# Expert weights of a pair side by side: 2 MB transfers, nine ring buffers, two one-time buffers

## The chip, the cores and the metric

The kernel runs on one core of a Trainium2 chip. The metric is device time in microseconds (us) of one execution. Seven units matter: TensorE (PE; PEld is its weight load), VectorE (DVE), ScalarE (ACT), GpSimd (POOL), SyncE (SP, which here only issues DMAs), and 16 DMA engines that all queues share.

## The reference, cut to what matters

One decoder layer over 576 tokens (512 prompt, 64 sample): a mixer, cross-attention, and a hierarchical mixture of experts, which is the part that is changed. All of it is float32.

```python
def hier_moe(x, w_gr, b_gr, w_er, b_er, w_e1, w_e3, w_e2):
    g_idx = argmax(x @ w_gr + b_gr)                  # one of 4 groups per token
    top_l, top_i = top_k(logits of the group's 8 experts, 2)
    gate = p_g * softmax(top_l)
    ...
    # per expert: (silu(xb @ w_e1[e]) * (xb @ w_e3[e])) @ w_e2[e]
    # rows are weighted by gate and added to their tokens
...
y = rmsnorm(h + hier_moe(rmsnorm(h, g3)), g_final)
```

There are 32 experts; w_e1 and w_e3 are 1024x512, w_e2 is 512x1024, so an expert has 6 MB of weights and all of them 192 MB (201 million bytes). With 576 tokens nearly every expert is used, and all are read.

## The kernel before, in words

Up to about 580 us the kernel computes mixer and cross-attention; the last projection (`w_co`, its weights in the tiles `wst`) runs from 518 to 578 us. Then it routes: logits, ranks, places (lines 1082 to 1274). The tile `more`, which says whether any expert overflows its 64 slots, is written at the end of that. Tokens are written to a DRAM table `rows_d`, and fetched back sorted by group with indirect DMAs (`fetch_rows`, line 1061) into `acc`, two tiles of 128 rows for each group; `acc` has room for two groups.

The experts run in 16 pairs of two (loop at line 1564), four pairs to a group. Of a pair p:

- `gather` (line 1493) makes X, the pair's tokens by features, with one-hot matmuls from `pthi`, `ptlo`, which `split_group` (line 1477) makes of the fetched rows: a rounded part on ACT and the rest on DVE, in four blocks of columns.
- First products, line 1575: 32 matmuls of X with w_e1 and w_e3 into two banks H. Each expert takes 64 of the 128 output rows, so the two experts' matmuls alternate. A matmul is two records in the profile.
- The gate, lines 1597 to 1600: Silu on ACT, a multiplication on DVE, into `sg`. TensorE turns `sg` (line 1603), ACT copies it (line 1607).
- Second products, line 1616: 16 matmuls with w_e2 into Y, which is split into `yhi`, `ylo`; `combine` (line 1528) adds them to `acc` through one-hot matmuls, one pair later.

Every four pairs a group is finished: final norm, and an indirect store to `y`. At pair 9 (`GENERAL`) stands a branch on `more` over code for overflowing experts, which the given inputs do not take.

Weights come through SP's queue in the order of use: 12 transfers of 1 MB for a pair (`load_one`, line 1308). Transfers 0 to 7 are the quarters of w_e1|w_e3, of one expert and then of the other; 8 to 11 the halves of w_e2. Each of the 128 partitions receives a row of 8 KB. They go into a ring of 18 buffers, 13 in the pool `wpa`, which is free from 518 us, and 5 in `wpb`, which is free when the last projection ends. The last three of the first 18 also wait for the first fetched rows (`i_first`). From then on a transfer waits until the products have read the buffer that it reuses. The last pair's w_e2 is loaded as four column blocks, each by two transfers of 512 KB in rows of 256 numbers (line 1328); the last pair is also worked off in these blocks, with the last norm between them (`last_norm`, line 1543).

A scheduler orders the instructions of each engine by their place in the program and by their dependences; `tc.issue_after(i)` keeps an instruction behind i on the engine's queue. An engine works its queue off in order. SP also reads `more` into a register (a TENSOR_LOAD, line 1448), at the place in its queue where the scheduler puts it.

In this text a **unit** is 2 MB of weights: the two experts' transfers of the same quarter or half. A pair has six units, the kernel 96, numbered 0 to 95. Before the change a unit is two transfers; the ring holds nine units.

Of the kernel before, what the change touches and what calls it, by code (L numbers as in the profile page):

```python
# [21 lines left out]
T = 576  # L22
# [5 lines left out]
CHUNK_A, CHUNK_B = 13, 5  # L28
PAY = 24
GENERAL = 9  # L30
CUT = 128
# [67 lines left out]
def _lay_out(inputs):  # L99
# [49 lines left out]
    w13 = np.concatenate([f["w_e1"][0], f["w_e3"][0]], 2).reshape(32, 4, 2, 128, 1024)  # L149
    a["w13"] = ca(w13.transpose(0, 1, 3, 2, 4)).reshape(32, 4, 128, 2048)  # L150
    w2 = f["w_e2"][0].reshape(32, 4, 128, 2, 512)
    a["w2"] = ca(w2.transpose(0, 3, 2, 1, 4)).reshape(32, 2, 128, 2048)
# [23 lines left out]
def body(ctx: ExitStack, tc: tile.TileContext, I, O, dbg=None):  # L176
# [847 lines left out]
    acc = keep.tile([128, 4, D], F32, name="acc")  # L1024
# [57 lines left out]
    with ExitStack() as st:  # L1082
        rp = pool(st, "route")
        space = acc.rearrange("p a c -> p (a c)")
        acc3, last = space[:, 0:T], space[:, T:2 * T]
        gp.memset(space[:, 2 * T:2048], 0.0)
        gp.memset(space[64:128, 3584:4096], 0.0)
        stage = [space[:, 2048 + i * 512:2560 + i * 512].rearrange("p (i c) -> p i c", c=128) for i in range(3)]
        stage4 = space[0:64, 3584:4096]
        hots = [space[:, a:a + 320].bitcast(BF16).rearrange("p (i c) -> p i c", c=128) for a in (2048, 3072)]  # L1090
# [115 lines left out]
        i_first = [fetch_rows(acc[:, t], src[:, t:t + 1]) for t in range(2)][-1]  # L1206
# [19 lines left out]
        posm = rt(5, 32)  # L1226
# [67 lines left out]
    def hp_():  # L1294
# [3 lines left out]
    HOMES = [(wpa, f"wa{i}") for i in range(CHUNK_A)] + [  # L1298
        (wpb, f"wb{i}") for i in range(CHUNK_B)]
# [3 lines left out]
    def wchunk():  # L1303
        home, tag = HOMES[len(ring) % RING]
        ring.append(home.tile([128, 2048], F32, name=f"wc{len(ring)}", tag=tag))
        return ring[-1]

    def load_one(p, n):

        w = wchunk()  # L1310
        if n < 8:
            q, h = divmod(n, 2)
            i_w = sy.dma_start(w, I["w13"][2 * p + h, q])
            if CHUNK_A + 2 < len(ring) <= RING:
                tc.add_manual_dep(i_w.ins, i_first.ins.name, mybir.DependencyInfo(
                    mybir.DependencyClass.Sync, mybir.DependencyReason.DATA), reason="the first rows before more weights")
            w = w.rearrange("p (k c) -> p k c", k=2)
            views[p, "in", q, h] = lambda k2, c: w[:, k2, c * 512:c * 512 + 512]
        elif p < 15:
            c, h = divmod(n - 8, 2)  # L1320
            sy.dma_start(w, I["w2"][2 * p + h, c])
            w = w.rearrange("p (j c) -> p j c", j=4)
            views[p, "out", c, h] = lambda j: w[:, j]
        else:
            c = n - 8
            w = w.rearrange("p (h j c) -> p h j c", h=2, j=4)
# [32 lines left out]
    loads_to(RING)  # L1359
# [40 lines left out]
    def dense(Xe, sv, e, add):  # L1400
        def piece(x):
            w = mw.tile([128, 512], F32, name="piece", tag="sq")
            gp.dma_start(w, x.rearrange("e p c -> p (e c)"))
            return w

        H = [cp_(), cp_()]
        for k in range(KT):
            for c in range(2):
                at = k % 2 * 1024 + c * 512
                pe.matmul(H[c], lhsT=Xe[:, k], rhs=piece(I["w13"][bass.ds(e, 1), k // 2][:, :, at:at + 512]), start=(k == 0),  # L1410
                          stop=(k == KT - 1))
# [7 lines left out]
        for c in range(2):  # L1419
            Y = cp_()  # L1420
            for j in range(4):
                pe.matmul(Y, lhsT=sg[:, j * 128:j * 128 + 128],
                          rhs=piece(I["w2"][bass.ds(e, 1), c][:, :, j * 512:j * 512 + 512]), start=(j == 0), stop=(j == 3))
            add(slice(c * 512, c * 512 + 512), Y)

    def redo(g, data, index):
# [11 lines left out]
        ve.tensor_copy(g8.rearrange("p (j c) -> p j c", c=2),  # L1438
                       data[:, 8:20].rearrange("p (j c) -> p j c", c=3)[:, :, 1:3])
        with tc.For_i(0, 8) as j:  # L1440
            sv = mw.tile([128, 2], F32, name="gsv")
            ve.tensor_copy(sv[:, 0:1], data[:, 8:9])
            ve.tensor_copy(sv[:, 1:2], g8[:, bass.ds(j, 1)])
            dense(Xe, sv, j + 8 * g, lambda cs, Y: ve.tensor_tensor(ax[:, cs], ax[:, cs], Y, op=OP.add))
# [32 lines left out]
    def split_group(g):  # L1477

        pt = [mw.tile([128, 2, D], F32R, name=n) for n in ("pthi", "ptlo")]
        for b in range(4):  # L1480
            cs = slice(b * 256, b * 256 + 256)
            split_tile(acc[:, 2 * g % 4:2 * g % 4 + 2, cs], pt[0][:, :, cs], pt[1][:, :, cs])
# [45 lines left out]
    def combine(y, oT, p, cs, after=None):  # L1528
# [3 lines left out]
        for c in range(2):  # L1532
# [3 lines left out]
            a = acc[:, p // 4 * 2 % 4 + c, cs]  # L1536
# [4 lines left out]
    tail_s = mw.tile([128, 8], F32, name="tail_s").rearrange("p (i c) -> p i c", c=4)  # L1541

    def last_norm(c, cs):
        a, s = acc[:, 2 + c], tail_s[:, c]
        sq = mw.tile([128, 512], F32, name="sq")[:, 0:cs.stop - cs.start]
# [6 lines left out]
        else:  # L1552
# [3 lines left out]
            gp.tensor_scalar(a[:, 0:CUT], a[:, 0:CUT], r, None, op0=OP.mult)  # L1556
            ac.activation(a[:, CUT:512], a[:, CUT:512], AF.Copy, scale=r)
# [5 lines left out]
    so, done, nxt = None, None, None  # L1563
    for p in range(16):
        if p == 0:
            gather(0, oh, X, range(4))
        if p % 4 == 0 and p != GENERAL - 1 or p % 4 == 3 and p < 15:
            nxt = slots_of(p // 2 + 1), tokens_x()
        so = scales(p, oh)
        H = [hp_(), hp_()]  # L1570
        at = p % 2 * 128
        for k in range(KT):
            for c in range(2):
                for e in range(2):
                    i_h = pe.matmul(H[c][rows[e]], lhsT=X[:, k, at + e * 64:at + e * 64 + 64],  # L1575
                                    rhs=views[p, "in", k // 2, e](k % 2, c), start=(k == 0), stop=(k == KT - 1))
        sv, oT = so
        with tc.issue_after(i_h.ins):
            if done:
                combine(*done, slice(0, D if p == GENERAL else 512))  # L1580
# [7 lines left out]
            if p % 4 == 3 and p < 15:  # L1588
                split_group(p // 4 + 1)
# [6 lines left out]
        sg = mw.tile([128, 512], F32, name="sg")  # L1596
        ac.activation(sg, H[0], AF.Silu, scale=sv[:, 0:1])  # L1597
        if p == 15:
            tc.keep_in_program_order(ac.preload_act_table_set("natural_log_exp_and_others"))
        ve.scalar_tensor_tensor(sg, H[1], sv[:, 1:2], sg, op0=OP.mult, op1=OP.mult)  # L1600
        ps = xp_()
        for j in range(4):
            pe.transpose(ps[:, j * 128:j * 128 + 128], sg[:, j * 128:j * 128 + 128], ident)  # L1603
        if done and p != GENERAL:
            combine(*done, slice(512, D))
        hT_ = sg.rearrange("p (a b) -> p a b", a=4)
        ac.activation(sg, ps, AF.Copy)
        y = [mw.tile([128, D], F32R, name=name) for name in ("yhi", "ylo")]
        n = 4 if p == 15 else 2
# [34 lines left out]
```

## Time and profile before

| | us |
|---|---|
| median of 3 runs | 1074.18 (1073.82 to 1074.52) |
| the profiled execution | 1077.59 |
| its span, first to last instruction | 1075.9 |
| mean granted TensorE clock | 0.974 of full |

The prediction sums against the profiled execution; its time lies 3.41 us above the median. Reading: first the 40 slices of the page, to see which resource is full in which stretch; then the windows of single stretches; then the rows of engines where something waits. Times in rows are us from the span's start.

### The profile page before, as it was taken

The numbers are of one execution on the slowest core, as the hardware profiler recorded it, in microseconds if no ns is written. First come the engines' busy times: TensorE is split into PE (matmuls) and PEld (weight loads), VectorE is DVE, ScalarE is ACT, GpSimd is POOL, SyncE is SP. The second block draws the span as 40 slices with busy tenths as digits, with TensorE's granted clock in tenths as the row PEclk, the third lists the DMA queues.
The fourth block names the chain that finished last, engine by engine and source line by source line (L and its number), as shares of the span: only waits on it lengthen the run. The fifth ranks groups of instructions, "written<-read, shape, count | busy, mean of one in ns | idle before, by whom it ended". The sixth has DMA issues, their size and how long they took to land. (4 is left out here: it accounts for less than half of the span.)

```text
span 1075.9 us, 17992 instructions
## 1 busy us (share of the span) xinstructions
PE 1020.5 (95%) x7375; PEld 713.3 (66%) x7375; DVE 455.1 (42%) x1043; ACT 341.0 (32%) x695; POOL 62.6 (6%) x87
## 2 busy tenths in 40 slices
PE   8999899999999999999996799999899969999996
PEld 7999889986769999888996444354335334444333
DVE  6337785456554754555334325223322322222113
ACT  5356313467443533333322112113211311122103
POOL 2100010000000200000111000001000000001002
PEclk9999999999999999999997799999899989999998
DMA  7312115836785753665693799999999999999993
GB/s 258 119 41 79 43 44 186 310 90 235 264 287 187 254 189 96 216 215 198 253 371 131 267 419 421 420 422 421 420 420 420 420 417 422 421 421 421 421 406 127
DMA packets 59674, 300.46 MB, mean 279 GB/s; under 512 B 7288, under 2 KB 13929, under 8 KB 35136
## 3 DMA queue, kind: packets, MB, share of 16 engines
q1 hardware_dynamic: 53856, 282.66, 68.0%
q0 software_dynamic: 5120, 16.28, 4.2%
q8 instruction: 59, 0.97, 0.4%
q10 hardware_dynamic: 608, 0.30, 0.1%
q14 instruction: 31, 0.25, 0.1%
HBM read 290.30 MB, written 12.19 MB: 281 GB/s over the span
## 5 line engine op out<-in xcount | busy, mean ns | idle before, releaser
L1575 PE MATMUL hp<-wc,X 128*64 128x512 f32 x1024 | 242.1, 595 | 5.3 <-DMA wc<-w 5.2
L1575 PEld LDWEIGHTS hp<-wc,X 128*64 128x64 f32 x1024 | 89.2, 137 | 149.3 <-issue 131.1
L283 PE MATMUL pj<-hi,whi 128*128 128x288 f32 (+1 forms) x544 | 162.8, 300 | 1.3 <-DVE hT L903 0.8
L283 PE MATMUL pj<-hi,wlo 128*128 128x288 f32 (+1 forms) x544 | 161.7, 297 | 0.0
L283 PE MATMUL pj<-lo,whi 128*128 128x288 f32 (+1 forms) x544 | 161.6, 298 | 0.0
L1616 PE MATMUL hp<-wc,sg 128*64 128x512 f32 (+1 forms) x544 | 122.2, 577 | 0.1
L234 ACT ACTIVATE whi<-wst 128x1024 fp32r<-128x1024 f32 (+1 forms) x62 | 65.6, 1058 | 127.8 <-PE pj L283 101.1
L283 PEld LDWEIGHTS pj<-hi,whi 128*128 128x128 f32 x544 | 102.8, 189 | 4.6 <-issue 1.8
L283 PEld LDWEIGHTS pj<-lo,whi 128*128 128x128 f32 x544 | 102.9, 189 | 2.1 <-issue 1.4
L283 PEld LDWEIGHTS pj<-hi,wlo 128*128 128x128 f32 x544 | 102.9, 189 | 1.3 <-issue 1.2
L235 DVE TENSOR_TENSOR wlo<-wst,whi 128x1024 fp32r<-128x1024 f32 (+1 forms) x62 | 76.1, 1227 | 42.7 <-ACT whi L234 42.6
L1616 PEld LDWEIGHTS hp<-wc,sg 128*64 128x64 f32 x544 | 39.1, 138 | 70.2 <-issue 65.6
L1600 DVE SCALAR_TENSOR_TENSOR sg<-hp,sv,sg 128x512 f32<-128x512 f32 x16 | 12.0, 749 | 170.9 <-PE hp L1575 170.9
L1597 ACT ACTIVATE sg<-hp,sv 128x512 f32<-128x512 f32 x16 | 11.0, 687 | 195.0 <-PE hp L1575 195.0
L1537 DVE TENSOR_TENSOR acc<-acc,cp 128x512 f32<-128x512 f32 (+1 forms) x66 | 42.5, 667 | 60.5 <-PE cp L1535 60.1
L244 DVE TENSOR_TENSOR ylo<-hp,yhi 128x512 fp32r<-128x512 f32 (+1 forms) x34 | 22.4, 659 | 73.8 <-ACT yhi L243 71.8
L308 PE MATMUL pj<-whi,hi 128*128 128x256 f32 (+1 forms) x184 | 52.3, 284 | 0.0
L308 PE MATMUL pj<-whi,lo 128*128 128x256 f32 (+1 forms) x184 | 52.1, 283 | 0.0
L308 PE MATMUL pj<-wlo,hi 128*128 128x256 f32 (+1 forms) x184 | 52.0, 283 | 0.0
L243 ACT ACTIVATE yhi<-hp 128x512 fp32r<-128x512 f32 (+1 forms) x34 | 19.4, 572 | 84.1 <-PE hp L1616 82.4
L1501 PE MATMUL xp<-oh,pthi 128*128 128x256 f32 x128 | 35.2, 308 | 10.3 <-DVEq L1449 7.1
L283 PE MATMUL pj<-h1lo,whi 128*128 128x288 f32 x128 | 38.8, 303 | 0.0
(441 smaller groups left out, 1648.4 us busy)
## 6 DMA issues: line engine op xcount, KB each, us to landing
wc<-w SPq DMA_DIRECT2D x188, 1024.0 KB, 19.8
kv<-kc SPq DMA_DIRECT2D x16, 768.0 KB, 7.0
kv<-vc SPq DMA_DIRECT2D x16, 768.0 KB, 6.0
ckv<-mkc SPq DMA_DIRECT2D x16, 512.0 KB, 4.9
ckv<-mvc SPq DMA_DIRECT2D x16, 512.0 KB, 5.1
wst<-w_qkb SPq DMA_DIRECT2D x8, 512.0 KB, 3.6
wst<-w_mk SPq DMA_DIRECT2D x8, 512.0 KB, 4.9
wst<-w_mv SPq DMA_DIRECT2D x8, 512.0 KB, 4.5
```

The source lines that it names most:

```text
L234: ac.activation(hi[:, s], w[:, s], AF.Copy)
L235: ve.tensor_tensor(lo[:, s], w[:, s], hi[:, s].bitcast(F32), op=OP.subtract)
L243: ins = ac.activation(hi, x, AF.Copy)
L244: ve.tensor_tensor(lo, x, hi.bitcast(F32), op=OP.subtract)
L283: pe.matmul(p, lhsT=a[:, k], rhs=b[k][:, c], start=(k == 0 and s == 0), stop=(k == KT - 1 and s == 2))
L308: pe.matmul(outs[i][0:m], lhsT=a[xk][:, i * 128:i * 128 + m], rhs=b[:, k, :], start=(kh == 0 and k == 0 and s == 0 and head), stop=(kh == ...
L1501: pe.matmul(ps[:, k * 256:k * 256 + 256], lhsT=pt[s][:, c, kk * 128:kk * 128 + 128], rhs=oh[:, c], start=(k + c + s == 0), stop=(k + c + s ...
L1537: ve.tensor_tensor(a, a, ps, op=OP.add)
L1575: i_h = pe.matmul(H[c][rows[e]], lhsT=X[:, k, at + e * 64:at + e * 64 + 64], rhs=views[p, "in", k // 2, e](k % 2, c), start=(k == 0), stop ...
L1597: ac.activation(sg, H[0], AF.Silu, scale=sv[:, 0:1])
L1600: ve.scalar_tensor_tensor(sg, H[1], sv[:, 1:2], sg, op0=OP.mult, op1=OP.mult)
L1616: i_y = pe.matmul(Y[rows[e]], lhsT=hT_[:, j, rows[e]], rhs=views[p, "out", c, e](j), start=(j == 0), stop=(j == 3))
```

## The change

The host lays the weights of a pair's two experts side by side, so that a unit is one transfer of 2 MB with a row of 16 KB per partition. The ring has nine homes of one unit: six in `wpa`, one cut in two 1 MB halves (`wah` in `wpa`, `wbh` in `wpb`), two in `wpb`. Unit 0 is loaded into two one-time buffers: `w_first`, which takes the place of the second half of `acc` until group 1 is fetched, and `wsecond`, in a buffer of X. So ten units are loaded ahead instead of nine. The routing's scratch tiles move out of `acc`, and two GpSimd memsets go.

The load order is changed at the end: the first-product units of pairs 14 and 15 come first, then the second-product units of 14, then of 15, whose four column blocks now lie contiguous in `w2l` (rows of 8 KB). Pair 15's first products are computed inside pair 14. `split_group` for the next group, called at pairs 3, 7 and 11, is tied behind the gate computed last at that point (pairs 2, 6, 10). In the last norm ACT scales all of 0:512 instead of 128:512, and GpSimd's share (0:128) goes. `general` follows the new layout; it is not run.

```diff
-CHUNK_A, CHUNK_B = 13, 5
+UNITS_A, UNITS_B = 6, 2
...
-CUT = 128
...
+    w13 = np.concatenate([f["w_e1"][0], f["w_e3"][0]], 2).reshape(16, 2, 4, 2, 128, 1024)
+    a["w13"] = ca(w13.transpose(0, 2, 4, 1, 3, 5)).reshape(16, 4, 128, 4096)
+    w2 = f["w_e2"][0].reshape(16, 2, 4, 128, 2, 512)
+    a["w2"] = ca(w2.transpose(0, 4, 3, 1, 2, 5)).reshape(16, 2, 128, 4096)
+
+    a["w2l"] = ca(a["w2"][15].reshape(2, 128, 2, 4, 2, 256).transpose(0, 4, 1, 2, 3, 5)).reshape(4, 128, 2048)
...
-    acc = keep.tile([128, 4, D], F32, name="acc")
+    def group_rows():
+        return keep.tile([128, 2, D], F32, name="acc", bufs=2)
+    w_first = keep.tile([128, 2048], F32, name="wfirst", tag="acc", bufs=2)
+    accs = [group_rows()]
...
-    HOMES = [(wpa, f"wa{i}") for i in range(CHUNK_A)] + [
-        (wpb, f"wb{i}") for i in range(CHUNK_B)]
+    HOMES = [(wpa, f"wa{i}") for i in range(UNITS_A)] + [None] + [(wpb, f"wb{i}") for i in range(UNITS_B)]
...
+    order = [(p, n) for p in range(14) for n in range(6)] + [(p, n) for ns in (range(4), range(4, 6)) for p in (14, 15)
+                                                             for n in ns]
...
+    def first_loads():
+        first = [w_first, mw.tile([128, 2048], F32, name="wsecond", tag="X", bufs=2), None]
+        load(0, first, (0,))
+        for i in range(1, UNITS_A + 1):
+            load(i, whome())
+        split = whome()
+        load(UNITS_A + 1, split, (0,))
+        ins = load(0, first, (1,))
+        with tc.issue_after(ins.ins):
+            ins = load(UNITS_A + 1, split, (1,))
+        for i in range(UNITS_A + 2, RING + 1):
+            with tc.issue_after(ins.ins):
+                ins = load(i, whome())
+            tc.add_manual_dep(ins.ins, i_first.ins.name, mybir.DependencyInfo(
...
-            gp.tensor_scalar(a[:, 0:CUT], a[:, 0:CUT], r, None, op0=OP.mult)
-            ac.activation(a[:, CUT:512], a[:, CUT:512], AF.Copy, scale=r)
+            ac.activation(a[:, 0:512], a[:, 0:512], AF.Copy, scale=r)
...
-            if p % 4 == 3 and p < 15:
-                split_group(p // 4 + 1)
+            if p % 4 == 3:
+                with tc.issue_after(i_gate[0].ins), tc.issue_after(i_gate[1].ins):
+                    split_group(p // 4 + 1)
...
+        sg = gated(p, H, sv)
+        if p == 14:
+            loads_to(len(order))
+            with tc.issue_after(i_h.ins):
+                so15 = scales(15, oh)
+                H15, i_h = first_products(15, X)
...
+    for c in range(4):
+        i_y = second_products(15, c, 256, sgT, y)
+        with tc.issue_after(i_y.ins):
+            if c == 0:
+                combine(*done, slice(0, D))
+            elif c == 1:
+                combine(y, oT, 15, slice(0, 512), last_norm)
+            elif c == 3:
+                combine(y, oT, 15, slice(512, 768), last_norm)
+                combine(y, oT, 15, slice(768, D), last_norm)
```

What this moves is shown at three places.

SP's queue, where the units that are loaded ahead end. Before (`wc13` is the 14th transfer of 1 MB, in `wpb`):

```order
L1313 DMA wc13_6732<-w13 128x2048
L1313 DMA wc14_6734<-w13 128x2048
L1313 DMA wc15_6736<-w13 128x2048
L1313 DMA wc16_6738<-w13 128x2048
L1313 DMA wc17_6740<-w13 128x2048
L1448 TENSOR_LOAD more_5907
L1313 DMA wc18_6962<-w13 128x2048
```

And now (`wc5` is unit 6, `wh6` the halves of unit 7, `wc7` to `wc9` units 8 to 10):

```order
L1329 DMA wc5_6718<-w13 128x4096
L1332 DMA wh6_6720<-w13 128x2048
L1485 TENSOR_LOAD more_5908
L1332 DMA wsecond_6706<-w13 128x2048
L1332 DMA wh6_6721<-w13 128x2048
L1329 DMA wc7_6725<-w13 128x4096
L1329 DMA wc8_6727<-w13 128x4096
L1329 DMA wc9_6950<-w2 128x4096
```

The read of `more` stood behind all that is loaded ahead; now 6 MB of it stand behind the read, the second half of unit 0 first.

ACT's queue in pairs 1 and 2 (`pthi` is the split of the next group, `X` the gather, the first `sg` row the gate, the second the copy). Before, from pair 1's gate on:

```order
L1597 ACTIVATE sg<-hp,sv 128x512
L243 ACTIVATE pthi<-acc 128x2x256
L1507 ACTIVATE X<-xp,gmoe 128x256 x2
L243 ACTIVATE pthi<-acc 128x2x256
L1607 ACTIVATE sg<-xp 128x512
L243 ACTIVATE pthi<-acc 128x2x256 x2
L1523 ACTIVATE oT<-xp 128x256
```

And now:

```order
L1617 ACTIVATE sg<-hp,sv 128x512
L1544 ACTIVATE X<-xp,gmoe 128x256 x2
L1682 ACTIVATE sg<-xp 128x512
L1560 ACTIVATE oT<-xp 128x256
L245 ACTIVATE yhi<-hp 128x512 x2
L1617 ACTIVATE sg<-hp,sv 128x512
L245 ACTIVATE pthi<-acc 128x2x256 x4
L1682 ACTIVATE sg<-xp 128x512
```

The four splits left pair 1 and stand behind pair 2's gate, ahead of its copy; pairs 5 and 6, 9 and 10 read alike.

TensorE's queue at the end. Before, from pair 15's turn of `sg` on (second products 64x256, `cp` is `combine`):

```order
L1603 MATMUL xp<-ident,sg 128x128 x4
L1535 MATMUL cp<-yhi,oT 128x512
L1535 MATMUL cp<-ylo,oT 128x512
L1616 MATMUL hp<-wc_11187,sg 64x256
...
L1616 MATMUL hp<-wc_11187,sg 64x256 x7
L1616 MATMUL hp<-wc_11190,sg 64x256 x8
L1616 MATMUL hp<-wc_11193,sg 64x256
L1535 MATMUL cp<-yhi,oT 128x512 x2
L1535 MATMUL cp<-ylo,oT 128x512 x2
L1616 MATMUL hp<-wc_11193,sg 64x256 x7
L1616 MATMUL hp<-wc_11196,sg 64x256 x8
```

And now, from the last first products of pair 15 (`wc_12004`) and its turn on; `wc_12006`, `wc_12071` are pair 14's second-product units, `wc_12073`, `wc_12076` pair 15's:

```order
L1608 MATMUL hp<-wc_12004,X 64x512 x8
L1626 MATMUL xp<-ident,sg 128x128 x4
L1639 MATMUL hp<-wc_12006,sg 64x512 x8
L1639 MATMUL hp<-wc_12071,sg 64x512 x8
L1639 MATMUL hp<-wc_12073,sg 64x256 x8
...
L1639 MATMUL hp<-wc_12073,sg 64x256 x3
...
L1639 MATMUL hp<-wc_12073,sg 64x256 x5
L1639 MATMUL hp<-wc_12076,sg 64x256
...
L1639 MATMUL hp<-wc_12076,sg 64x256 x15
```

Behind the first eight of pair 15's second products stands one half of pair 14's `combine`, behind the next three the other, and behind the first of `wc_12076` the first `combine` of pair 15.

## Rows read from the trace of the kernel before

**Rows 1.** The page's 40 slices of the span: DMA share, and rate.

```profile
DMA  7312115836785753665693799999999999999993
GB/s 258 119 41 79 43 44 186 310 90 235 264 287 187 254 189 96 216 215 198 253 371 131 267 419 421 420 422 421 420 420 420 420 417 422 421 421 421 421 406 127
```

**Rows 2.** The page's chain that ended last, by line.

```profile
DMA wc<-w 13%; PE hp L1575 2%; PE hp L1616 1%; PE xp L1501 1%; PE cp L1535 0%; POOL acc L1556 0%; POOLq L1640 0%; ACT sq L1547 0%; POOL o_y L1367 0%; ACT X L1507 0%; PE xp L1519 0%; PE xp L1603 0%; DVE ylo L244 0%; DVE acc L1537 0%; ACT yhi L243 0%
```

**Rows 3.** Who waited for whom: us in total, times, longest (TensorE for weights).

```profile
PEld hp L1575 <- DMA wc<-w: 15.5, 17, 2.0
```

**Rows 4.** Windows: busy us of each engine, clock, DMA share, GB/s (start).

```profile
608.00:612.00 4.00, 4.00 (x21) 1.42 (x22) 0.32 (x2) 0.39 (x1) 0.00 (x0) 1.00 0.27 41
612.00:616.00 4.00, 4.00 (x22) 1.36 (x20) 0.00 (x0) 0.00 (x0) 0.00 (x0) 1.00 0.98 416
```

**Rows 5.** SP's timeline: issues of units 9, 10 and 13 (start, us).

```profile
609.99 0.34 SPq L1313 DMA_DIRECT2D wc<-w  x1
...
613.42 0.33 SPq L1321 DMA_DIRECT2D wc<-w  x1
...
629.46 0.80 SPq L1313 DMA_DIRECT2D wc<-w  x2
```

**Rows 6.** Windows of full DMA: rows of 6, 4, 8 and 1 KB.

```profile
187.00:190.00 3.00, 3.00 (x25) 3.00 (x24) 1.53 (x4) 1.52 (x5) 0.00 (x0) 1.00 1.02 422
...
463.00:466.00 3.00, 2.98 (x13) 2.50 (x14) 0.88 (x4) 0.60 (x1) 0.00 (x0) 1.00 1.02 410
...
900.00:1000.00 100.00, 98.24 (x480) 45.98 (x478) 25.22 (x47) 20.33 (x39) 2.82 (x2) 1.00 1.01 421
...
1048.00:1056.00 8.00, 7.63 (x32) 3.32 (x34) 3.03 (x5) 2.57 (x3) 0.00 (x0) 1.00 1.05 343
```

**Rows 7.** The page's DMA queues: instruction fetch (packets, MB, share of 16 engines).

```profile
q8 instruction: 59, 0.97, 0.4%
```

**Rows 8.** Timelines at the start: DVE, ACT, TensorE; then line 1448 on SP.

```profile
592.21 0.17 DVE L1273 CAST more<-rt 128x9 int32<-128x9 f32 x1
...
596.43 2.19 ACT L243 ACTIVATE pthi<-acc 128x512 fp32r<-128x512 f32 x4 [6.17 <-DMA acc<-rows_d,src]
...
598.26 0.55 PE L1501 MATMUL xp<-oh,pthi 128*128 128x256 f32 x1 [3.21 <-DVE oh L1489]
...
601.95 1.97 PE L1575 MATMUL hp<-wc,X 128*64 128x512 f32 x2
...
L1448 SPq TENSOR_LOAD <-more x1: 476/476/476, 598.2 to 598.2; - x1
```

**Rows 9.** Timelines in pair 5: ACT's and TensorE's weight loads, with idle time before.

```profile
762.21 0.63 ACT L243 ACTIVATE pthi<-acc 128x512 fp32r<-128x512 f32 x1 [8.01 <-DMA acc<-rows_d,src]
...
763.62 0.93 PEld L1519 LDWEIGHTS xp<-pay,oh 128*128 128x128 f32 x4 [5.12 <-ACT X L1507]
```

**Rows 10.** Window at the end of the weight stream.

```profile
1056.00:1060.00 4.00, 3.53 (x32) 2.15 (x28) 1.10 (x3) 0.77 (x2) 0.00 (x0) 1.00 0.31 105
```

**Rows 11.** The chain that ended last, in order of time (start, us, what).

```profile
1048.35 3.65 PE hp L1575 x12
...
1053.13 0.44 PE xp L1603 x4
...
1059.64 1.21 PE cp L1535 x4
1060.85 3.60 PE hp L1616 x30
1064.44 0.45 PE cp L1535 x2
```

**Rows 12.** Timelines of ACT and POOL in the tail.

```profile
1068.13 0.60 ACT L1557 ACTIVATE acc<-acc,tail_s 128x384 f32<-128x384 f32 x1
1068.18 1.90 POOL L1556 TENSOR_SCALAR acc<-acc,tail_s 128x128 f32<-128x128 f32 x2 [3.51 <-ACT tail_s L1555]
1070.24 1.04 POOL L1367 DMA_INDIRECT o_y<-acc,dst  x1 [0.16 <-POOL acc L1556]
```

More of the change, by code (lines that the diff above doesn't have):

```diff
@@ L1083, in body @@
         rp = pool(st, "route")
[L1084 to L1090, printed above, removed]
+        space = accs[0].rearrange("p a c -> p (a c)")
+        acc3, last = rpool.tile([128, T], F32, name="R1"), rp.tile([128, T], F32, name="last")
+        stage = [space[:, i * 512:i * 512 + 512].rearrange("p (i c) -> p i c", c=128) for i in range(3)]
+        stage4 = space[0:64, 1536:2048]
+        hots = [x[:, 0:320].bitcast(BF16).rearrange("p (i c) -> p i c", c=128) for x in (acc3, last)]
         idb = rp.tile([128, 5, 2], BF16, name="idb")
@@ new lines, in whome @@
+    def whome():
+        i = len(ring)
+        home = HOMES[i % RING]
+        if home:
+            w = home[0].tile([128, 4096], F32, name=f"wc{i}", tag=home[1])
+            ring.append([w[:, 0:2048], w[:, 2048:4096], w])
+        else:
+            ring.append([x.tile([128, 2048], F32, name=f"wh{i}", tag=t) for x, t in ((wpa, "wah"), (wpb, "wbh"))] + [None])
+        return ring[-1]
+    order = [(p, n) for p in range(14) for n in range(6)] + [(p, n) for ns in (range(4), range(4, 6)) for p in (14, 15)
+                                                             for n in ns]
@@ new lines, in load @@
+        return out
+    loaded = [0]
+    def loads_to(n):
+        n = min(n, len(order))
+        for i in range(loaded[0], n):
+            load(i, whome())
+        loaded[0] = max(loaded[0], n)
+    def first_loads():
+        first = [w_first, mw.tile([128, 2048], F32, name="wsecond", tag="X", bufs=2), None]
+        load(0, first, (0,))
+        for i in range(1, UNITS_A + 1):
+            load(i, whome())
+        split = whome()
[7 more added lines that the diff above has]
+            tc.add_manual_dep(ins.ins, i_first.ins.name, mybir.DependencyInfo(
+                mybir.DependencyClass.Sync, mybir.DependencyReason.DATA), reason="the first rows before more weights")
+        loaded[0] = RING + 1
@@ L1541, in body @@
     tail_s = mw.tile([128, 8], F32, name="tail_s").rearrange("p (i c) -> p i c", c=4)
+    junk = []
     def last_norm(c, cs):
-        a, s = acc[:, 2 + c], tail_s[:, c]
-        sq = mw.tile([128, 512], F32, name="sq")[:, 0:cs.stop - cs.start]
+        a, s = accs[3][:, c], tail_s[:, c]
+        if not junk:
+            junk.append(tokens_x().rearrange("p a b -> p (a b)"))
+        sq = junk[0][:, c * D + cs.start:c * D + cs.stop]
         part = {0: 0, 512: 1, 768: 2}[cs.start]
@@ L1562, in body, with first_products @@
     split_group(0)
[L1563 to L1569, printed above, removed]
+    def first_products(p, X):
         H = [hp_(), hp_()]
```

163 lines of the change are left out of this document (88 added, 75 removed).

## The prediction

> **What bounds the kernel now.** The 40 slices come first. From slice 24 to the last but one the DMA share reads 9 and the rate about 421 GB/s [rows 1]; before that nothing is full for long. So from about 612 us the kernel runs at the pace of its weight stream. The chain that ended last agrees: its largest part, 13%, is the arrival of weights, and the next largest have 2% [rows 2]. TensorE, busy in name, waits for weights: 17 times at the first products, 15.5 us in all [rows 3]. Whatever makes TensorE, ACT or DVE faster between 640 and 1030 us is therefore worth nothing unless the stream ends sooner.
>
> The stream begins as follows. Eighteen transfers are loaded ahead. From 608 to 612 us the DMA engines are nearly idle, 0.27 with 41 GB/s, and from 612 us they are full [rows 4]. Unit 9, the first that reuses a buffer, is issued at 609.99 us [rows 5], when TensorE has read unit 0. The 41 GB/s of that window are 0.16 MB, or 0.4 us at 421 GB/s; so the stream flows from 611.6 us, 1.6 us behind the issue. It ends near 1057.2 us: the last window still has a share of 0.31 of 4 us [rows 10]. A unit (2.097 MB) takes 4.98 us at 421 GB/s.
>
> **The change, part by part.**
>
> *Two one-time buffers.* They put unit 9 ahead of the stream, which looks like 4.98 us. The nine homes are as many as before, so unit 10 still waits until unit 1 is read: 613.42 us [rows 5], flowing from 615.0 us. Units 10 to 12 then last until 630.0 us. Unit 13 waits for pair 0's second products, 629.46 us [rows 5], and flows from 631.1 us. Before, units 9 to 12 filled 611.6 to 631.5 us and unit 13 followed without a gap. So the gain is 631.5 - 631.1 = **0.4 us**: the DMA now idles 1.1 us there, because TensorE has not freed a home. After unit 13 TensorE frees a unit every 3.4 us (613.42 - 609.99) in first products, less than 4.98, and no further gap follows.
>
> *The start.* SP reads `more` ahead of 6 MB of first loads. `more` is written at 592.4 us; the read takes 0.48 us [rows 8], with its register work about 1 us by my estimate, so the second half of unit 0 is issued near 593.5 us and lands near 598 us (1.6 us to flow, 2.5 us for 1 MB), while TensorE starts first products at 601.95 us [rows 8]. That cover is 4 us. If the read is as late as before (598.2 us), the half lands at about 603 us and costs 1 to 2 us. It also flows beside the first fetched rows, for which ACT waits until 596.43 us; that costs up to 1 us. Against it, the one-hot tiles on DVE, for which TensorE waited until 598.26 us, now stand ahead of the split on DVE's queue; the first of ACT's four splits is ready at 597.0 us (a quarter of 2.19 us), so no more than some 0.8 us of those 1.3 can be won once DVE has done its part of it. I take 0, with -0.8 and +2 as ends. The projection weights `wst` now queue behind larger transfers, but SP issues them a tile or more ahead of their use. The GpSimd memsets and the scratch tiles cost nothing: the routing waits for DVE.
>
> *Rows of 16 KB.* Of the 83 units from 13 on, nine go into the cut home and the last two in halves, all with rows of 8 KB as before; 72 get 16 KB rows. No row shows such a packet in this queue. Per DMA engine the full windows give, for rows of 1, 4, 6 and 8 KB, 47.8, 160, 233 and 311 ns [rows 6] (16 engines x bytes / rate). A line through 1 and 8 KB is 10.1 ns + 37.6 ns per KB; 4 KB lies on it, 6 KB 3 ns below. By it 16 KB take 612 ns against 622 for two of 8 KB: 1.6%. From 6 to 8 KB alone the rate does not rise at all (422 and 421), so the other end is 0%. I take 1.3%, nearer to the line because three of four sizes lie on it: about 427 GB/s, 72 x 4.98 x 0.013 = **4.7 us** (ends 0 and 5.7). The Trainium skill (DMA: Bandwidth & Descriptors, Where 436 GB/s comes from) has a port ceiling of 435 GB/s, which leaves room for that. The same page (Rules for kernel authors) asks for 128 partitions and at least 1 MiB per DMA, which the kernel before already has; by it larger transfers win nothing, and that is the first rival below.
>
> *Half as many issues and completions.* SP is idle anyway: nothing. Eight transfers in flight are now up to 16 MB instead of 8, within the ring's 18.
>
> *The last unit pair.* Before, the last 4.19 MB came in rows of 1 KB at 343 GB/s, 12.2 us; at 421 they take 10.0 us: **2.2 us**.
>
> *The end.* Before, 7.2 us passed from the end of the stream (1057.2) to the last second products, 1064.44 us [rows 11], because pair 15's first products had just been released at 1048.35 us. Now pair 15's first products land some 20 us before the end. They take 3.65 us, and their gate and turn 1.6 us (1052.0 to 1053.57) [rows 11]; pair 14's second products follow, and from its second unit on, which lands 10.0 us before the end, TensorE has: that unit 3.4, four blocks of pair 15 at 1.9 (16 of the 30 records in 3.60), three combines at 1.2, and about 0.5 of waiting for splits: 15.2 us. So it ends 5.2 us behind the stream: **2.0 us** gained.
>
> *The last norm.* GpSimd's two pieces take 1.90 us and release the first store at 1070.24 us [rows 12]. ACT's piece takes 0.60 us for 384 columns [rows 12], about 0.65 for 512; the pieces of both tiles follow the four small operations. I estimate the first store 1.0 us earlier: **1.0 us**, by 0.4 either way.
>
> *The splits.* In pair 5 ACT stood 8.01 us before a split whose rows had not arrived, and the gather's copies behind it held TensorE for 5.12 us [rows 9]. Behind pair 6's gate the rows are there. TensorE wins 5 us and gives them back to the next wait for weights: **0** at the end. The cover is the full stream (421 GB/s from 900 to 1000 us [rows 6], and so from 700 on [rows 1]). In pairs 2, 6 and 10 the copy of `sg` is now queued behind four splits (2.19 us at the start [rows 8]); while it waits, TensorE turns and combines.
>
> Sum: 0.4 + 0 + 4.7 + 2.2 + 2.0 + 1.0 = 10.3 us. The profiled execution would take 1077.59 - 10.3 = 1067.3 us. The median lies 3.41 us below that execution, so I forecast **1063.9 us**.
>
> **The rivals.**
>
> 1. *Longer rows win nothing.* 6 KB and 8 KB run at the same rate [rows 6]; the step from 1 to 4 KB speaks against it. 10.3 - 4.7 = 5.6 us: 1068.6 us. Chance 0.22.
> 2. *TensorE sets the end.* If the start loses its 2 us, or pair 9's branch (over more code now) holds TensorE longer, the faster stream finds it late. For it: TensorE counts as busy for 98.24 of the 100 us from 900 on [rows 6], which leaves little margin. Against it: a unit takes 3.4 us of TensorE and 4.98 of the stream, and TensorE waited 17 times for weights [rows 3]. Two to three us lost: about 1066.5 us. Chance 0.11.
> 3. *Slower: long rows fall behind.* One mechanism: a 16 KB packet holds its DMA engine longer than two of 8 KB. The trace has one kind of packet of that size, instruction fetch: 59 packets with 0.97 MB take 0.4% of 16 engines' span [rows 7], or 1.2 us each, twice the 0.61 of the line. That is another queue, squeezed in beside the stream, so it is weak evidence. The change breaks even when a unit takes 5.6 / 72 = 0.08 us more than 4.98, a rate of 414.5 GB/s; at 400 GB/s it would lose 72 x 0.26 = 19 us and end near 1087 us. At the fetch's price the stream would nearly double. Chance 0.06.
> 4. *Nothing moves.* The stream's gains are eaten by more idle DMA between 631 and 700 us, where TensorE frees the homes: within 2 us of 1074.2. The rates there speak against it: the margin grows by 1.5 us with each unit. Chance 0.03.
>
> **How the numbers follow.** The forecast has 0.58. About 0.2%, 2 us, is what a measurement of this kernel can tell from no change. Forecast and rivals 1 and 2 are faster, 0.91; rival 4 is no change, 0.03; rival 3 is slower, 0.06. The lower end takes the line's 1.6% (1.0 us more), 0.8 us at the start and 1 us more in the tail: 1061.1, and I write 1060.5. The upper end holds rival 1 with 1.4 us lost: 1070.0.
>
> **What would show it.** Right: the windows from 700 to 1000 us read 425 to 429 GB/s with about half the packets; DMA idles about 1 us near 630 us and not again; the second half of unit 0 is issued near 593.5 us; TensorE no longer waits 5 us in pair 5, but waits longer for weights later; the last second products end 5 us behind the last landing; no 1 KB window at the end. Wrong: 421 GB/s as before (rival 1), first products of pair 15 that wait for X or the gate and not for weights (rival 2), or a DMA share of 1 at a rate under 415 GB/s (rival 3).

## The result, and the profile after

| | before | changed |
|---|---|---|
| median | 1074.52 us (1073.82 to 1076.93, 5 runs) | 1068.87 us (1066.94 to 1069.39, 5 runs) |
| ratio, 95% interval | | 0.9938 (0.9925 to 0.9951) |
| the profiled execution | 1077.59 us, span 1075.9 | 1069.27 us, span 1067.6 |

The change makes the kernel faster by 6.7 us (5.3 to 8.1), where I forecast 10.3 and 1063.9 us. The time lies inside the range, and next to rival 1 (1068.6 us), though not for that rival's reason: the long rows did win what I gave them. The upper end of the range had been set by rival 1, so that the range holds the time is in part luck. Medians and ratios in this text leave out three slow runs, one each of `halves` (1981.28 us), `big_8k` (1648.51 us) and `end_both` (3227.09 us).

First the 40 slices of the changed kernel, DMA share and rate, which answer to [rows 1], its chain that ended last, which answers to [rows 2], and how TensorE waited for weights at the first products, which answers to [rows 3]:

```profile
DMA  7312114826775752656692899999999999999992
GB/s 260 119 41 80 43 44 165 335 73 234 279 283 183 264 185 89 209 206 215 254 366 109 313 408 427 426 427 425 427 425 425 427 419 427 427 425 426 427 424 114
...
PE 10%; DMA 7%; ACT 0%; DVE 0%; issue 0%; POOLq 0%; DVEq 0%; POOL 0%; SPq 0%
DMA wc<-w 7%; PE hp L1608 4%; PE hp L1639 4%; PE xp L1538 1%; PE cp L1572 1%; PE xp L1556 0%; PE xp L1626 0%; DVEq L1720 0%; POOLq L1720 0%; PE xp L1559 0%; POOL o_y L1403 0%; DVE X L1546 0%; DVE acc L1574 0%; ACT X L1587 0%; ACT X L1544 0%
...
PEld hp L1608 <- DMA wc<-w: 23.2, 13, 3.2
```

The stream is as full as before, at 425 to 427 GB/s where it was 421. In the chain, weights have 7% where they had 13%, and TensorE 10%. TensorE still waits for weights, 23.2 us in all where it was 15.5.

Now the windows that answer to [rows 4, 6, 10]: the gap ahead of the reused buffers, the gap near 630 us, the full stream, and its end in steps of 2 us.

```profile
610.00:612.00 2.00, 2.00 (x12) 0.72 (x10) 0.00 (x0) 0.00 (x0) 0.00 (x0) 1.00 0.08 33
612.00:614.00 2.00, 2.00 (x12) 0.65 (x10) 0.00 (x0) 0.00 (x0) 0.00 (x0) 1.00 1.04 270
...
628.00:632.00 4.00, 4.00 (x22) 1.29 (x18) 0.69 (x1) 0.60 (x1) 0.20 (x1) 1.00 0.93 345
...
900.00:1000.00 100.00, 97.62 (x486) 43.41 (x484) 28.25 (x52) 23.02 (x45) 2.82 (x2) 0.98 1.01 427
...
1040.00:1042.00 2.00, 0.98 (x6) 0.34 (x6) 0.69 (x1) 0.60 (x1) 0.00 (x0) 1.00 1.01 422
1042.00:1044.00 2.00, 2.00 (x12) 0.70 (x10) 0.00 (x0) 0.00 (x0) 0.00 (x0) 1.00 0.93 389
1044.00:1046.00 2.00, 2.00 (x18) 1.03 (x16) 0.42 (x1) 0.60 (x1) 0.00 (x0) 1.00 0.83 348
1046.00:1048.00 2.00, 2.00 (x14) 1.07 (x11) 1.18 (x3) 0.38 (x1) 0.00 (x0) 1.00 0.46 193
1048.00:1050.00 2.00, 2.00 (x12) 1.07 (x10) 1.25 (x3) 0.00 (x0) 0.00 (x0) 1.00 0.12 49
1050.00:1052.00 2.00, 1.53 (x13) 0.78 (x11) 0.96 (x3) 0.38 (x1) 0.00 (x0) 1.00 0.01 4
```

The gap near 630 us is there, though shorter than forecast: from 624 to 633 us the DMA engines idle about 0.7 us in all, where I had 1.1. No window of 1 KB rows is left. The end is not sharp: the share sinks over some 8 us. By its area the stream ends at 1042 + 2 x (0.93 + 0.83 + 0.46 + 0.12 + 0.01) = 1046.7 us.

Last, single instructions: DVE's cast of `more` and TensorE's first products, which answer to [rows 8], ACT's split for group 2, which answers to [rows 9], and in the tail the last wait for weights (it is unit 93, pair 14's second w2 unit), the last second products in the chain, and the first store, which answer to [rows 11, 12].

```profile
591.41 0.16 DVE L1278 CAST more<-rt 128x9 int32<-128x9 f32 x1
...
599.94 1.07 PE L1608 MATMUL hp<-wfirst,X 128*64 128x512 f32 x2
...
775.55 2.18 ACT L245 ACTIVATE pthi<-acc 128x512 fp32r<-128x512 f32 x4
...
1041.25 0.20 PEld L1639 LDWEIGHTS hp<-wc,sg 128*64 128x64 f32 x4 [1.90 <-DMA wc<-w]
...
1053.23 3.60 PE hp L1639 x30
...
1061.96 1.01 POOL L1403 DMA_INDIRECT o_y<-acc,dst  x1 [5.13 <-DVE acc L1597]
```

The first products come 8.53 us after the cast (9.74 before). The splits in pair 6 wait for nothing. From the landing of unit 93 to the last second products, at 1056.83 us, pass 15.6 us; before, from the landing of pair 15's last first-product unit at 1048.35 to 1064.44 us, 16.1 us [rows 11].

The work ahead of the experts shifts a profile by some us that no edit here touches: the cast of `more` falls between 589.18 and 594.35 us in the profiles below. So I set single profiles against each other from that cast. From there to the end of the span the changed kernel takes 476.2 us, the kernel before 483.7.

### The profile page after: what moved, and what is told of

It reads as the page before. It is cut to its first block, busy times and chain, and to the rows that moved or that the text cites. A ratio compares the mean times of both kernels' runs of the same rounds, so it can differ in the third digit from the quotient of the medians.

```text
span 1067.6 us, 17812 instructions
## 1 busy us (share of the span) xinstructions
PE 1009.1 (95%) x7375; PEld 702.0 (66%) x7375; DVE 454.1 (43%) x1043; ACT 340.9 (32%) x695; POOL 59.5 (6%) x83
## 5 line engine op out<-in xcount | busy, mean ns | idle before, releaser
L1608 PE MATMUL hp<-wc,X 128*64 128x512 f32 x912 | 206.5, 601 | 13.2 <-DMA wc<-w 13.2
L1608 PEld LDWEIGHTS hp<-wc,X 128*64 128x64 f32 x912 | 67.4, 139 | 147.3 <-issue 119.7
L1639 PE MATMUL hp<-wc,sg 128*64 128x512 f32 (+1 forms) x480 | 102.5, 567 | 1.1 <-DMA wc<-w 1.0
L1639 PEld LDWEIGHTS hp<-wc,sg 128*64 128x64 f32 x480 | 33.8, 137 | 60.5 <-issue 56.0
L246 DVE TENSOR_TENSOR ylo<-hp,yhi 128x512 fp32r<-128x512 f32 x30 | 20.7, 691 | 70.5 <-ACT yhi L245 70.5
L245 ACT ACTIVATE yhi<-hp 128x512 fp32r<-128x512 f32 x30 | 17.9, 597 | 78.8 <-PE hp L1639 78.8
```

The lines of the kernel that those rows point to most:

```text
L245: ins = ac.activation(hi, x, AF.Copy)
L246: ve.tensor_tensor(lo, x, hi.bitcast(F32), op=OP.subtract)
L1639: i_y = pe.matmul(Y[rows[e]], lhsT=sgT[:, j, rows[e]], rhs=views[p, "out", c, e](j), start=(j == 0), stop=(j == 3))
```

## The experiments

Each edit is one of the changed kernel. Differences to it are those of the two ratios to the kernel before, times 1074.5 us, with the intervals combined.

### Rows: 8 KB, in transfers of 1 MB and of 2 MB

`halves` loads each unit by two transfers; `big_8k` by one, from experts that lie apart in DRAM.

```diff
-            if w[2] is not None:
-                out = sy.dma_start(w[2], x)
-            else:
-                for h in halves:
+            for h in halves:
...
+                out = sy.dma_start(w[2].rearrange("p (h c) -> p h c", h=2), x.rearrange("h p c -> p h c"))
```

> The changed kernel with every unit loaded as two transfers of 1 MB, each with rows of 8 KB, in the same order and into the same homes. Theory A (long rows make the stream faster): the full windows fall from 424-427 GB/s back to about 421, and 72 units cost 72 x 4.98 x 0.013 = 4.7 us more, so about 1073.5 us and not clearly faster than the kernel before. Rival (the faster stream has another cause, such as the side-by-side layout or the chip of that day): 426 GB/s and 1069 us as the changed kernel. On the tail: if long rows spread the ends of the DMA engines, the fall of the rate at the end of the stream, 8.4 us wide in the changed kernel (the engines stop between 1042.2 and 1050.6 us), is narrower here, about 4 us; if the spread is there with any row, it stays at 7 to 9 us.

> The changed kernel with one transfer of 2 MB a unit as there, but the two experts apart in DRAM as in the kernel before, so that each of the 128 partitions gets two rows of 8 KB. Theory A (the length of the row counts): 421 GB/s in the full windows and about 1073.5 us, as with two transfers of 1 MB. Rival (the size of the transfer, or half as many completions, counts): 426 GB/s and about 1069 us.

Measured: `halves` 1073.89 us, ratio 0.9986 (0.9975 to 0.9997); `big_8k` 1073.66 us, 0.9990 (0.9980 to 1.0000): 5.2 and 5.6 us above the changed kernel, each within 1.8. The same window of `halves` and then of `big_8k`:

```profile
900.00:1000.00 100.00, 98.03 (x468) 47.18 (x466) 27.55 (x51) 22.29 (x43) 2.82 (x2) 1.00 1.01 421
...
900.00:1000.00 100.00, 96.32 (x474) 43.36 (x472) 27.54 (x51) 22.30 (x43) 2.82 (x2) 0.98 1.01 421
```

Both are back at 421 GB/s. It is the length of the row that counts, not the size of the transfer: theory A. And `halves`, which keeps all other parts of the change, is only 1.5 us (0.3 to 2.7) faster than the kernel before, where I had 5.6 us for those parts. That is what I missed. The end of the stream sinks about as slowly with rows of 8 KB as with rows of 16 KB (in `halves` the share falls from 0.98 in the window from 1048 us to 0.02 in that from 1056 us), so long rows are not the cause of that.

### The tie of the splits: with 16 KB and with 8 KB

```diff
-                with tc.issue_after(i_gate[0].ins), tc.issue_after(i_gate[1].ins):
-                    split_group(p // 4 + 1)
+                split_group(p // 4 + 1)
```

> The changed kernel with the splits of the next group no longer tied behind the gate. Forecast (the stalls lie beside the full stream): within 1 us of the changed kernel; ACT waits some 8 us for fetched rows before a split in pair 5, as in the kernel before, and TensorE some 5 us behind it. Rival (the stall in pair 5 delays the release of homes): up to 5 us slower, and windows with a DMA share under 0.95 after 770 us.

> The changed kernel with every unit loaded as two transfers of 1 MB in rows of 8 KB, and the splits no longer tied behind the gate. Theory (the fetched rows and the stores to y take turns with the weights packet by packet on each DMA engine, so that rows of 16 KB double what they wait; the tie is worth 11 us only beside such rows): ACT waits 7 to 13 us for fetched rows before a split in pair 5, not the 20.6 us of the untied kernel with rows of 16 KB; the stream stays full, and the time is that of the tied kernel with rows of 8 KB, 1073 to 1076 us. Rival (the tie is needed in the new order of the program whatever the rows): 11 us slower than that kernel, about 1085 us, with the gap in the stream after 900 us.

Measured: `untied` 1079.76 us, ratio 1.0043 (1.0028 to 1.0059), 11.3 us (9.1 to 13.5) slower than the changed kernel and slower than the kernel before; `halves_untied` 1073.82 us, 0.9982 (0.9969 to 0.9994), the same as `halves`. So my forecast failed for `untied` and the theory for `halves_untied` held. Pair 5 in `untied`, then in `halves_untied` (ACT's first split and the weight loads that stand behind it):

```profile
772.89 0.63 ACT L245 ACTIVATE pthi<-acc 128x512 fp32r<-128x512 f32 x1 [20.61 <-DMA acc<-rows_d,src]
774.30 0.93 PEld L1556 LDWEIGHTS xp<-pay,oh 128*128 128x128 f32 x4 [17.71 <-ACT X L1544]
...
761.79 0.63 ACT L245 ACTIVATE pthi<-acc 128x512 fp32r<-128x512 f32 x1 [11.22 <-DMA acc<-rows_d,src]
763.20 0.93 PEld L1553 LDWEIGHTS xp<-pay,oh 128*128 128x128 f32 x4 [8.33 <-ACT X L1541]
```

8.33 us lie beside the stream. 17.71 us and a second stall of 9.8 us in pair 9 do not: in the whole of `untied` TensorE waits for no weights, where in the changed kernel it did so for 23.2 us at the first products. Its spare time is used up, so TensorE and no longer the stream sets the pace to the end; homes are freed late, and the stream runs dry. The first stall also leaves TensorE at the lower of its two clocks: it stands from 756.6 to 774.30 us, and from 760 to 780 us the granted clock is 0.50 (1.2 of 2.4 GHz), against 1.00 in the changed kernel. How the 11.3 us divide between stalls and clock was not worked out.

```profile
880.00:900.00 20.00, 4.13 (x19) 3.96 (x20) 1.54 (x3) 2.81 (x4) 0.94 (x1) 0.65 1.01 418
900.00:920.00 20.00, 19.17 (x95) 9.58 (x96) 5.16 (x10) 4.98 (x10) 0.00 (x0) 0.93 0.76 307
```

Why the rows come later shows the view of DMA issues from 735 to 790 us, with the median time to landing in us: of `halves`, then of the changed kernel. (`big_8k`, which has rows of 8 KB in transfers of 2 MB, has 9.9 and 9.8.)

```profile
o_y<-acc,dst POOLq DMA_INDIRECT x2, 9.7
acc<-rows_d,src POOLq DMA_INDIRECT x2, 9.7
...
o_y<-acc,dst POOLq DMA_INDIRECT x2, 13.3
acc<-rows_d,src POOLq DMA_INDIRECT x2, 13.2
```

Stores and fetches of 128 rows of 4 KB take 3.6 and 3.5 us longer beside rows of 16 KB, and the fetches wait for the stores. (The kernel before has 9.8 and 8.1 us, but issues its two fetches 3.2 us apart, and not 1.4 us as here.) The sizes fit engines that take turns between the queues. By my estimate, such a transfer is 8 rows for each of 16 engines, and a weight row lasts 0.30 us longer. If each row waits for one weight row, the first of two transfers is held up by 2.4 us more and the second, behind it, by 4.8: 3.6 us at the median of the two. No view shows the single turns. The Trainium skill (DMA: Bandwidth & Descriptors, Queues, rings and completion order) says that an engine goes round the queues and empties one packet before it turns to the next; the trace agrees in so far as the delay grows with the row.

### Rows of 32 KB

Units 38 to 83 go two at a time into neighbouring homes, eight from there on; unit 1 takes the cut home. `rows_32k_late` also moves group 3's fetch. The diff shows the parts that matter.

```diff
+            if w[3] is not None:
+                out = sy.dma_start(w[3], x) if n % 2 == 0 else None
...
-            if p % 4 == 1 and 4 < p < 12:
-                fetch_group(p // 4 + 1)
+            if p == 5:
+                fetch_group(2)
...
                 gather(p // 2 + 1, *nxt, range(4))
+                fetch_group(3)
```

> The changed kernel with units 38 to 83 loaded two at a time, 4 MB a transfer with a row of 32 KB per partition, into pairs of neighbouring homes (eight homes from there on). By the line of the packet costs (10.1 ns and 37.6 ns a KB) a row of 32 KB takes 1213 ns against 1224 for two of 16 KB: 0.9%, about 431 GB/s, and 46 units x 4.92 x 0.009 = 2.0 us, so about 1066.8 us. Rival (16 KB is where the rows stop to pay, 427 GB/s being all there is): 426 GB/s and 1069 us; slower than that if homes that come free in twos let the stream run dry (windows with a DMA share under 0.98 after 700 us).

> The kernel with rows of 32 KB for units 38 to 83, with the fetch of group 3's rows moved behind pair 9's branch and gather. In the kernel with rows of 32 KB DVE stood 32.0 us in pair 9 until those rows had landed, and the stream dried up (0.16 of the DMA share from 900 to 920 us). Theory (long rows hold up the fetches, and nothing but that wait cost the 16 us): DVE no longer waits there, the rows land before the split behind pair 10's gate, the stream stays full at 430 to 432 GB/s in the windows with long rows, and 46 units x 0.9% give 2.0 us against the changed kernel: about 1067 us. Rival (homes that come free in twos make the stream run dry, whatever the fetch): as slow as the kernel with rows of 32 KB, about 1084 us, or between the two.

Measured: `rows_32k` 1084.54 us, ratio 1.0088 (1.0068 to 1.0108), the slow case, though not for the reason that the rival gave; `rows_32k_late` **1065.79 us, 0.9915 (0.9901 to 0.9930)**, faster than both kernels, by 2.5 us (0.4 to 4.6) against the changed one. First the stores and fetches from 840 to 905 us with their median time to landing, in the changed kernel and then in `rows_32k`; then, in `rows_32k`, DVE in pair 9, a window with long rows and the dry one.

```profile
o_y<-acc,dst POOLq DMA_INDIRECT x2, 13.9
acc<-rows_d,src POOLq DMA_INDIRECT x2, 13.9
...
o_y<-acc,dst POOLq DMA_INDIRECT x2, 20.6
acc<-rows_d,src POOLq DMA_INDIRECT x2, 21.4
...
900.15 0.88 DVE L1556 TENSOR_SCALAR X<-xp,gmoe 128x256 f32<-128x256 f32 x2 [32.03 <-DMA acc<-rows_d,src]
...
780.00:800.00 20.00, 15.76 (x68) 5.39 (x70) 5.58 (x12) 2.90 (x6) 0.00 (x0) 0.95 1.01 432
900.00:920.00 20.00, 18.85 (x78) 9.47 (x80) 4.11 (x9) 3.85 (x8) 0.00 (x0) 0.73 0.16 52
```

The rate does what the line says (432 GB/s), and the price is the same as above, once more larger: 6.7 and 7.5 us more to landing, where the same count with rows that last 0.60 us longer gives an estimate of 7.2. DVE stands 32.03 us in pair 9. With the fetch behind that place, in `rows_32k_late`:

```profile
876.07 0.88 DVE L1556 TENSOR_SCALAR X<-xp,gmoe 128x256 f32<-128x256 f32 x2 [1.24 <-PE xp L1548]
...
900.00:920.00 20.00, 19.66 (x96) 7.61 (x94) 8.01 (x15) 4.83 (x9) 0.00 (x0) 1.00 1.00 433
```

The wait is gone and the stream full. With the fetch moved the 16 us are back, so it was this wait that had cost them.

### The end

`rows_1k` loads the last two units in rows of 1 KB again; `end_before` restores the load order and the order of work of the last two pairs; `end_both` does both.

```diff
-                out = sy.dma_start(w[h], I["w2l"][2 * (n - 4) + h])
+                for e in range(2):
+                    out = sy.dma_start(w[h][:, e * 1024:e * 1024 + 1024].rearrange("p (j c) -> p j c", j=4),
+                                       I["w2"][p, n - 4].rearrange("p (e j c) -> p e j c", e=2, j=4)[:, e, :, h * 256:h * 256 + 256])
...
-    order = [(p, n) for p in range(14) for n in range(6)] + [(p, n) for ns in (range(4), range(4, 6)) for p in (14, 15)
-                                                             for n in ns]
+    order = [(p, n) for p in range(16) for n in range(6)]
...
-        if p == 14:
-            loads_to(len(order))
-            with tc.issue_after(i_h.ins):
-                so15 = scales(15, oh)
-                H15, i_h = first_products(15, X)
```

> The changed kernel with the load order and the order of work of the kernel before in the last two pairs (pair 15's first products after pair 14's second products), the contiguous column blocks kept. Theory A (units land by the slowest DMA engine, so the unit on which the tail rests lands at about 1041.3 us in either order, and TensorE has about 16 us behind it in either): within 1 us of the changed kernel, 1068 to 1070 us, second products ending about 10 us behind the mean end of the stream. Theory B (my forecast's step: the new order brings the end of TensorE 2.0 us nearer to the stream): 2 us slower than the changed kernel, about 1071 us.

> The changed kernel with the last two units (pair 15's column blocks) loaded in rows of 1 KB by transfers of 512 KB, as in the kernel before. My forecast's step (those rows cost 2.2 us of the stream, and the end follows the stream): 2.2 us slower than the changed kernel, about 1071 us. Theory A (TensorE has 15.6 us of work behind the landing of unit 93, pair 14's second w2 unit, and the last two units land within that time with either rows): no later than 0.5 us, 1068 to 1070 us, and from the landing of unit 93 to the last second products again 15 to 16 us.

> The changed kernel with the whole end of the kernel before: load order and order of work of the last two pairs, and the last two units in rows of 1 KB. By the two terms of my forecast 2.2 + 2.0 = 4.2 us slower than the changed kernel, about 1073 us. Theory A (TensorE has 15.6 to 16.1 us of work behind the landing of unit 93 in every case, which sets the end): at most 1 us slower, 1068 to 1070 us, and 16 us from the landing of unit 93 to the last second products.

Measured: `end_before` 1068.71 us, 0.9940 (0.9925 to 0.9955); `rows_1k` 1070.23 us, 0.9956 (0.9942 to 0.9971); `end_both` 1069.92 us, 0.9946 (0.9933 to 0.9959): 0.2, 1.9 and 0.9 us above the changed kernel, within 2.1, 2.1 and 2.0. The first two alone leave both readings open; the third excludes the 4.2 us of my two terms. The landing of unit 93 and the last second products, in `end_before`, `rows_1k` and `end_both`:

```profile
1042.69 0.20 PEld L1607 LDWEIGHTS hp<-wc,X 128*64 128x64 f32 x4 [2.16 <-DMA wc<-w]
1055.33 3.24 PE L1638 MATMUL hp<-wc,sg 128*64 128x256 f32 x26
...
1039.64 0.20 PEld L1641 LDWEIGHTS hp<-wc,sg 128*64 128x64 f32 x4 [2.01 <-DMA wc<-w]
1052.45 3.23 PE L1641 MATMUL hp<-wc,sg 128*64 128x256 f32 x26
...
1042.53 0.20 PEld L1609 LDWEIGHTS hp<-wc,X 128*64 128x64 f32 x4 [2.29 <-DMA wc<-w]
1055.18 3.24 PE L1640 MATMUL hp<-wc,sg 128*64 128x256 f32 x26
```

15.9, 16.0 and 15.9 us lie between them, as 15.6 and 16.1 in the changed kernel and the one before, and TensorE waits for no weights after that landing. The order of the last units and the length of their rows move these intervals by 0.5 us at most.

`cut` gives GpSimd its share (0:128) of the last norm back; it was run once.

> The changed kernel with GpSimd's share (0:128) of the last norm put back. From the end of the last second products to the first store of the last rows: 5.1 us in the changed kernel, 5.8 us in the kernel before. Forecast: 1.0 us longer here than in the changed kernel; by the two profiles 0.7 us, so 5.8 us.

```profile
1052.73 2.97 PE L1640 MATMUL hp<-wc,sg 128*64 128x256 f32 x24
...
1061.47 1.04 POOL L1403 DMA_INDIRECT o_y<-acc,dst  x1 [0.16 <-POOL acc L1596]
```

From 1055.70 to the store 5.8 us, against 5.1: the term is 0.6 us by these two profiles, not 1.0 (1068.81 us in that one run).

### The start

`single` has no one-time buffers; `late_oh` puts the first one-hot tiles back behind the split.

```diff
-        first = [w_first, mw.tile([128, 2048], F32, name="wsecond", tag="X", bufs=2), None]
-        load(0, first, (0,))
-        for i in range(1, UNITS_A + 1):
+        for i in range(UNITS_A):
...
-    oh, X = slots_of(0), tokens_x()
-    split_group(0)
+    X, n_low = tokens_x(), len(lows)
+    split_group(0)
+    with tc.issue_after(lows[n_low].ins):
+        oh = slots_of(0)
```

> The changed kernel without the two one-time buffers: unit 0 goes into the ring, nine units are loaded ahead and not ten. Theory (unit 13 waits for pair 0's second products in either case, so the unit ahead only buys idle DMA): the stream between 612 and 632 us has no gap, and the end is 0.4 to 1.1 us later than in the changed kernel, about 1069.7 us. Rival (a unit ahead is worth its time in the stream): 4.9 us later, about 1073.8 us.

> The changed kernel with the first one-hot tiles put back behind the first block of the split on DVE, as in the kernel before. In all profiles so far the first products start 9.74 us after the cast of more in the kernel before, and 8.52 to 8.53 us in those with the change. Theory (the one-hot tiles ahead of the split are that gain, and it moves the end): first products 9.6 to 9.9 us after that cast, unit 13 issued about 1.2 us later, end 0.8 to 1.2 us later. Rival (the rows' arrival sets it): first products at 8.5 us as now, nothing lost.

Measured: `single` 1067.92 us, 0.9942 (0.9926 to 0.9957), 0.4 us above the changed kernel, within 2.2, and from the cast to the end 476.5 against 476.2 us: that agrees with the 0.4 us forecast for the unit ahead and excludes the rival's 4.9. `late_oh` 1069.60 us, 0.9945 (0.9929 to 0.9961), 0.8 us above, within 2.2. Its edit did more than meant: all four splits came ahead of the one-hot tiles, and the first products started 12.96 us after the cast (604.71 - 591.75), 4.4 us later and not 1.2. From the cast the profile ends 1.25 us later. By proportion, the 1.2 us that the changed kernel wins at its first products are worth under half a microsecond at the end; the runs, within 2.2 us, do not show so small a part.

## Why the prediction was right or wrong

| step | forecast | measured |
|---|---|---|
| one-time buffers | 0.4 us | 0.4 (within 2.2); 0.3 by the profiles |
| start | 0 (-0.8 to +2 lost) | first products won 1.2, the end under 0.5 by proportion |
| rows of 16 KB | 4.7 | 5.2 and 5.6 (each within 1.8) |
| last unit pair, and the end | 2.2 + 2.0 | 0.9 together (within 2.0); 0.5 by the tail |
| last norm | 1.0 | 0.6 |
| splits | 0 | 0 (0.4 within 1.8) with rows of 8 KB, 11.3 (9.1 to 13.5) with 16 KB |

**Rows of 16 KB** were right in mechanism and size: 427 GB/s forecast, 425 to 427 measured. Rival 1, that longer rows win nothing, falls by `halves` and `big_8k`. The Trainium skill's rule from which it came (DMA: Bandwidth & Descriptors, Rules for kernel authors: 128 partitions and at least 1 MiB a DMA) is no bound here: with the same 2 MB a transfer, 8 KB rows give 421 GB/s and 16 KB rows 427, and 32 KB rows, in transfers of 4 MB, 428 to 433 in the windows of 20 us from 760 to 960 us of `rows_32k_late`, but for one of 423. None of these passes the same page's ceiling of 435 GB/s.

**Rivals 2 and 4.** TensorE does not set the end of the changed kernel, since it still waits for weights up to unit 93; it does so in `untied`. That nothing moves falls with the result.

**The step that failed is "The last unit pair" with "The end".** I let the end follow the stream's end, so that 2.2 us of faster rows and 2.0 us of better order could both be booked. The rows that I had at hand said otherwise: pair 15's first products were released at 1048.35 us and TensorE then worked to 1064.44 us [rows 11], 16.1 us, longer than the 12.2 us in which the last units came. In both kernels the end hangs on the landing of unit 93. In the changed kernel I put that landing 10.0 us ahead of the stream's end. It came 5.5 us ahead (1041.25 against 1046.7), since a unit is there when the slowest of 16 engines has brought its part, and the engines end some 8 us apart: the share sinks from 0.93 to 0.01, while in the trace each row of 8 KB still takes 0.31 us. The kernel before had shown this too: unit 93 should have been in at 1057.2 - 12.2 = 1045.0 us and landed at 1048.35. I used the landing for the one kernel and the mean for the other; that is the difference between the 2.0 us won that I booked and the 2.9 us lost behind the mean end of the stream (10.1 us against 7.2). Of these 4.9 us the landing has 4.5, and 0.4 are work behind it (15.6 us where I had 15.2).

**The splits** were booked at nothing, rightly for the change as it is; but the reason was half of it. The tie does not merely move a stall of 5 us that the stream hides. It is what lets the kernel have long rows at all: without it the change would have been slower than before (1.0043). Rival 3 looked for the price of long rows in the stream itself, and there it is none: a row of 16 KB takes less than two of 8 KB (427 GB/s against 421). The price falls on the stores and fetches that share the engines with the stream, which none of the prediction's rivals had.

**Start, buffers, norm**: the read of `more` ahead of 6 MB cost nothing that shows (the second half of unit 0 was issued at 592.64 us, forecast 593.5, and TensorE waited for neither half), the gap near 611 us came as worked out and that near 630 us shorter, and unit 13 was issued 2.3 us earlier counted from the cast (34.92 against 37.25 us). The norm's term was too large by 0.4 us. The measured parts, 0.4 + 0.5 (at most) + 5.4 + 0.9 + 0.6, sum to 7.8 us, inside 5.3 to 8.1. Between the two profiled executions the difference is 8.3, 0.8 of it from a cast of `more` that came earlier.

Open is why the engines drift apart. By the bytes still to come at each landing, units land some 0.4 of a unit behind the mean from 793 to 827 us in the changed kernel, 0.5 near 859 us and 0.9 from 982 us on. Two runs suggest that a pause undoes it, though none was made to test it. In `rows_32k`, whose stream had dried up near 900 us, unit 93 lands 0.4 of a unit behind, and the share ends with 0.81, 0.15 and 0.00 in steps of 2 us from 1064 us. In `untied`, which ran dry near 905 us, it ends with 0.99, 0.32 and 0.00 from 1052 us. What makes one engine slower than another no run shows.

## What to carry to other kernels

In this full weight stream the length of the row per partition set the rate even in transfers of 2 MB (421 GB/s with 8 KB, 427 with 16 KB); try 16 and then 32 KB, and at once look up every small transfer on another queue, because it lands later beside longer rows. What such a transfer feeds has to be tied to a later place first. And the last term of a sum should be counted from the landing on which the tail waits, in both kernels, not from the mean end of the stream.

## What the hardware showed that I had not expected

- Rows of 4 KB beside the stream: from 840 to 905 us, fetches landed in 10.2 us beside rows of 8 KB (`halves`), 13.9 beside 16 KB and 21.4 beside 32 KB.
- The line of the packet costs held beyond its points: it gives 612 and 1213 ns per row of 16 and 32 KB; 16 engines x 16 KB at 427 GB/s are 614 ns, and 16 x 32 KB at 432 GB/s are 1214 ns.
- At the end of a stream without a pause the engines stop up to 8 us apart, with rows of 8 KB about as with 16 KB. Where the last rows have 1 KB the end is sharper: in the kernel before, the share is 0.51, 0.12 and 0.00 in steps of 2 us from 1056 us.
